# Row-wise dot products of two 64 MB tensors and a softmax: the last step's loads cut into eleven staggered pieces, three loads merged or re-cut, one SyncE drain added

## The chip, the cores and the metric

The kernel runs on one core of one Trainium2 chip. The metric is the device time of one execution in microseconds (us); several runs are taken and the median is given. The engines that matter are VectorE (DVE), ScalarE (ACT), SyncE (SP, which issues nearly all transfers) and the core's 16 DMA engines, which carry data from device memory into on-chip memory. A tile is a block of on-chip memory with 128 partitions.

## The reference

```
B, N, D = 8, 4096, 512
gram = np.matmul(x, y.transpose(0, 2, 1))
diag = np.diagonal(gram, axis1=1, axis2=2)
diag = diag - diag.max(axis=-1, keepdims=True)
exp = np.exp(diag)
return (exp / exp.sum(axis=-1, keepdims=True)).astype(np.float32)
```

Only the diagonal of the product is used, so for each of 8 x 4096 rows one dot product of 512 float32 elements of x and of y is needed, and then a softmax over the 4096 values of each of the 8 batches. All of x and y (2 x 67.1 MB) must be read once; the output is 0.13 MB.

## The kernel before

**Layout.** Four batches make one half (Q = 4). Each batch of a half takes 32 partitions (G = 32), and each partition holds 128 consecutive rows of x or y (C = 128). So `diag[0]` and `diag[1]`, one for each half, are tiles of 128 partitions x 128 dot products. `diag[1]` has one column more for a partial maximum.

**Steps.** The work runs in S = 8 steps of R = 32 rows per partition (four steps to each half); a step's x or y is 128 x 32 x 512 floats, 8.39 MB. There are two buffers for x (`xs[0]`, `xs[1]`, in turn) and one for y (`ys`), which the next step's y overwrites. Everything is issued in the order of the program: the schedule is written out by hand, each engine takes its instructions in that order, and semaphores are put in where one instruction needs another's result. An instruction that needs two of them has a separate semaphore wait in front of it on its engine.

**Steps 0 to 5** (line 118 on). SP loads x (`load_x`, line 63) and then y (`load_y`, line 66); step 0's x comes as two transfers, of 2 and of 30 rows. ACT copies the last K = 6 rows of `ys` to the tile `side` (line 123), so that `ys` is free sooner. DVE multiplies x by y in place (`products`, line 70): 26 rows against `ys`, then 6 rows against `side`. DVE then sums the products along D for 30 rows (`sums`, line 73), and ACT does the last two rows (`sums_act`, line 78, an activation with an accumulator for each row). The loads are held by the buffers: the next step's y waits until the products have read `ys`, the x of the step after next waits until the sums have read its buffer. After step 3 the first half's exponentials are made (`exps`, line 99); `normalize` (line 107) stands in step 4.

**Step 6** (lines 133 to 139). x in one transfer, y in two halves of 16 rows, with `products` for each half; DVE sums the last 8 rows and ACT the first 24.

**Step 7**, the last (lines 141 to 150). x and y come in pieces of 16, 8, 4, 2, 1 and 1 rows, in turn x and y; x's last piece has the last two rows, so that there are eleven transfers. `dots` (line 83) makes one row's dot product in one DVE instruction with an accumulator, for each row as its pieces land. Ahead of the dots of row 30, `largest` (line 97) takes the maximum of the 126 columns that are done into the extra column of `diag[1]`.

**The end** (lines 152 to 158). SP stores the first half's result `res[0]` in four transfers of 32 partitions. `exps` takes the maximum of the last three columns (the two last dots and the partial maximum), exchanges it over each group of 32 partitions (`over_quadrant`, line 91), ACT makes the exponentials and their sum, `normalize` sums over the groups, inverts and multiplies, and ACT issues the last store.

**Semaphores of the transfers.** All transfers share eight completion semaphores in turn, so the n-th waits until the (n - 8)-th has landed. SP waits for that in its own queue, with everything behind it.

**Ahead of step 0** (lines 115 and 116) `addr_align` fills DVE's and ACT's programs with no-operations up to an aligned address (61 each in the trace).

Of the kernel before, what the change touches and what calls it, by code (L numbers as in the profile page):

```python
# [1 line left out]

# [5 lines left out]


@with_exitstack
def kernel(
    ctx: ExitStack,
    tc: tile.TileContext,
    x: bass.AP,
    y: bass.AP,
    out: bass.AP,
):
    nc = tc.nc
    ctx.enter_context(tc.manual_schedule())  # L20
    f32 = mybir.dt.float32
    Alu = mybir.AluOpType
    Act = mybir.ActivationFunctionType
    X = mybir.AxisListType.X
    B, N, D = x.shape
    P = nc.NUM_PARTITIONS
    G = 32
    Q = P // G
    C = N // G
    R = 32  # L30
    H = R // 2
    K = 6
    W = 2
    S = B // Q * (C // R)


    xv = x.rearrange("(s b) (j c) d -> s (b j) c d", b=Q, j=G)
    yv = y.rearrange("(s b) (j c) d -> s (b j) c d", b=Q, j=G)
    ov = out.rearrange("(s b) (j c) -> s (b j) c", b=Q, j=G)

    big = ctx.enter_context(tc.tile_pool(name="big", bufs=1))
    small = ctx.enter_context(tc.tile_pool(name="small", bufs=1))


    xs = [big.tile([P, R, D], f32, name=f"xs{i}") for i in range(2)]
    ys = big.tile([P, R, D], f32, name="ys")
    side = big.tile([P, K, D], f32, name="side")

    diag = [small.tile([P, C + i], f32, name=f"diag{i}") for i in range(B // Q)]
    res = [small.tile([P, C], f32, name=f"res{i}") for i in range(B // Q)]  # L50

    def columns(t, r0, n):
        c0 = t % (C // R) * R + r0
        return slice(c0, c0 + n)

    def rows(t, r0, n):
        return xs[t % 2][:, r0 : r0 + n, :]

    def dots_of(t, r0, n):
        return diag[t * R // C][:, columns(t, r0, n)]  # L60

    def load_x(t, r0, n):
        nc.sync.dma_start(out=rows(t, r0, n), in_=xv[t * R // C, :, columns(t, r0, n), :])  # L63

    def load_y(t, r0, n):
        nc.sync.dma_start(out=ys[:, r0 : r0 + n, :], in_=yv[t * R // C, :, columns(t, r0, n), :])  # L66

    def products(t, r0, n, yt):
        xt = rows(t, r0, n)
        nc.vector.tensor_tensor(out=xt, in0=xt, in1=yt, op=Alu.mult)  # L70

    def sums(t, r0, n):
        nc.vector.tensor_reduce(out=dots_of(t, r0, n), in_=rows(t, r0, n), axis=X, op=Alu.add)  # L73

    def sums_act(t, r0, n):
        for r in range(r0, r0 + n):
            row = xs[t % 2][:, r, :]
            nc.scalar.activation(out=row, in_=row, func=Act.Copy, accum_out=dots_of(t, r, 1))  # L78

    def dots(t, r0, n):  # L80
        for r in range(r0, r0 + n):
            xt = xs[t % 2][:, r, :]
            nc.vector.scalar_tensor_tensor(  # L83
                out=xt, in0=xt, scalar=1.0, in1=ys[:, r, :], op0=Alu.mult, op1=Alu.mult,
                accum_out=dots_of(t, r, 1),
            )

    def over_quadrant(name, column, op, negate=False):

        got = small.tile([P, 1], f32, name=name)  # L90
        nc.vector.tensor_reduce(  # L91
            out=got, in_=column.to_broadcast([P, G]), axis=X, op=op, negate=negate, apply_transpose=True
        )
        return got

    def largest(out, d):
        nc.vector.tensor_reduce(out=out, in_=d, axis=X, op=Alu.max)  # L97

    def exps(i, d):
        mxp = small.tile([P, 1], f32, name=f"mxp{i}")  # L100
        largest(mxp, d)
        nmx = over_quadrant(f"nmx{i}", mxp, Alu.max, negate=True)
        sump = small.tile([P, 1], f32, name=f"sump{i}")
        nc.scalar.activation(out=res[i], in_=diag[i][:, :C], func=Act.Exp, bias=nmx, scale=1.0, accum_out=sump)  # L104
        return sump

    def normalize(i, sump):
        total = over_quadrant(f"sum{i}", sump, Alu.add)
        rc = small.tile([P, 1], f32, name=f"rc{i}")
        nc.vector.reciprocal(out=rc, in_=total)  # L110
        nc.vector.tensor_single_scalar(out=res[i], in_=res[i], scalar=rc, op=Alu.mult)  # L111

    nc.vector.addr_align(128, offset=0, max_nops=255)
    nc.scalar.addr_align(128, offset=0, max_nops=255)

    for t in range(S - 2):
        if t == 0:
            load_x(t, 0, 2)  # L120
        load_x(t, 2 if t == 0 else 0, R - 2 if t == 0 else R)
        load_y(t, 0, R)
        nc.scalar.activation(out=side, in_=ys[:, R - K :, :], func=Act.Copy)  # L123
        if t == C // R:
            normalize(0, sump)
        products(t, 0, R - K, ys[:, : R - K, :])
        products(t, R - K, K, side)
        sums(t, 0, R - W)
        sums_act(t, R - W, W)
        if t == C // R - 1:  # L130
            sump = exps(0, diag[0])

    t = S - 2
    load_x(t, 0, R)
    for r0 in (0, H):
        load_y(t, r0, H)
        products(t, r0, H, ys[:, r0 : r0 + H, :])
    sums(t, R - H // 2, H // 2)
    sums_act(t, 0, R - H // 2)

    t += 1
    r0 = 0
    for n in (16, 8, 4, 2, 1, 1):
        if r0 < R - 1:
            load_x(t, r0, max(n, 2))
        load_y(t, r0, n)
        if r0 == R - 2:
            largest(diag[1][:, C:], diag[1][:, : C - 2])
        dots(t, r0, n)
        r0 += n  # L150

    met = small.tile([P, C - R], f32, name="met")
    nc.scalar.activation(out=met, in_=diag[1][:, : C - R], func=Act.Copy)  # L153

    for p, n in ((0, G), (G, G), (2 * G, G), (3 * G, G)):
        nc.sync.dma_start(out=ov[0, p : p + n, :], in_=res[0][p : p + n, :])
    normalize(1, exps(1, diag[1][:, C - 2 :]))
    nc.scalar.dma_start(out=ov[1], in_=res[1])


# [1 line left out]
_INS = ['x', 'y']  # L162
_OUTS = [((8, 4096), 'float32')]


# [23 lines left out]
```

## Time and profile before

| what | value |
|---|---|
| time, median of 3 runs | 320.78 us (320.74 to 320.86) |
| profiled execution: span from first to last instruction | 318.9 us |
| time outside the span (median less span) | 1.9 us |
| bytes read from device memory | 134.22 MB, 421 GB/s over the span |
| DVE busy | 244.7 us (77%), 96 instructions |
| ACT busy | 42.0 us (13%), 84 instructions |
| longest idle of DVE for one cause | 66.5 us in 6 waits, for y |

The span is that of one execution, taken by the hardware profiler; time within it is counted from its first instruction. A line such as `L83 DVE SCALAR_TENSOR_TENSOR xs<-xs,ys 128x512` gives the code line, the engine, the operation, the tiles written and read and their shape. "SPq" is SP's queue: the time there is that of issuing a transfer, not of the transfer.

### The profile page before, as it was taken

The page shows a single profiled execution, that of the slowest core. Times are in us where ns is not written, and L with a number is a line of the kernel's source. Part 1 is how long each engine was busy: PE and PEld are TensorE (multiplying, and loading weights), DVE is VectorE, ACT ScalarE, POOL GpSimd, SP SyncE. Part 2 cuts the span into 40 slices and gives each one's busy share as a digit, 9 for nine tenths or more (in the row PEclk, how much of TensorE's full clock was granted, in tenths as well). Part 3 has the DMA queues.
Part 4 walks back from the last instruction along what each step waited for, and adds up shares of the span by engine and source line. Part 5 has one row for each costly group of instructions (what it writes and reads, how often), then busy time and mean ns, then how long its engine had stood idle before and what let it go on. Part 6 is the DMA issues. An engine that isn't in the chain of part 4 may idle for free.

```text
span 318.9 us, 424 instructions
## 1 busy us (share of the span) xinstructions
DVE 244.7 (77%) x96; ACT 42.0 (13%) x84; POOL 0.2 (0%) x4
## 2 busy tenths in 40 slices
DVE  0000069995899939999399994999949999996995
ACT  1000030100301003010120103000030100197000
POOL 0000000000000000000000000000000000000000
DMA  8999999999999999999999999999999899999993
GB/s 344 463 395 493 411 395 493 427 395 427 477 411 395 460 460 395 395 518 403 395 501 419 395 444 477 395 395 518 403 395 493 362 452 419 444 427 415 419 413 117
DMA packets 4226, 134.37 MB, mean 421 GB/s; under 512 B 512, under 2 KB 768, under 8 KB 1536
## 3 DMA queue, kind: packets, MB, share of 16 engines
q1 hardware_dynamic: 4080, 134.29, 97.9%
q10 hardware_dynamic: 144, 0.07, 0.1%
q14 instruction: 2, 0.02, 0.0%
HBM read 134.22 MB, written 0.13 MB: 421 GB/s over the span
## 4 chain that ended last, share of the span: by engine, by line
DMA 62%; DVE 35%; issue 2%; SPq 0%; ACT 0%; DVEq 0%
DMA ys<-in_y_dram 62%; DVE xs L70 30%; DVE diag L73 4%; DVE xs L83 0%; SPq L63 0%; DVE res L111 0%; DVE nmx L91 0%; DVE sum L91 0%; ACT res L104 0%; DVE rc L110 0%; DVE mxp L97 0%; DVEq L70 0%; SPq L66 0%; DVEq L83 0%
## 5 line engine op out<-in xcount | busy, mean ns | idle before, releaser
L70 DVE TENSOR_TENSOR xs<-xs,ys 128x13312 f32<-128x13312 f32 (+1 forms) x8 | 101.4, 12690 | 66.5 <-DMA ys<-in_y_dram 66.5
L73 DVE TENSOR_REDUCE diag<-xs 128x30 f32<-128x15360 f32 (+1 forms) x7 | 101.3, 14476 | 0.2
L78 ACT ACTIVATE xs<-xs 128x512 f32<-128x512 f32 x36 | 22.2, 617 | 111.0 <-DVE xs L70 111.0
L123 ACT ACTIVATE side<-ys 128x3072 f32<-128x3072 f32 x6 | 16.6, 2763 | 121.7 <-DMA ys<-in_y_dram 121.7
L83 DVE SCALAR_TENSOR_TENSOR xs<-xs,ys 128x512 f32<-128x512 f32 x32 | 19.9, 685 | 3.4 <-DMA ys<-in_y_dram 3.3
L70 DVE TENSOR_TENSOR xs<-xs,side 128x3072 f32<-128x3072 f32 x6 | 20.1, 3351 | 0.0
L78 ACT ACTIVATION_READ_ACCUMULATOR xs<-xs 128x1 f32 x36 | 6.7, 187 | 0.0
L104 ACT ACTIVATE res<-diag,nmx 128x128 f32<-128x128 f32 x2 | 0.8, 402 | 37.6 <-DVE nmx L91 37.6
L83 DVE DVE_READ_ACCUMULATOR xs<-xs,ys 128x1 f32 x32 | 2.6, 80 | 0.0
L123 ACT ACT_TABLE_LOAD x1 | 1.3, 1283 | 3.4 <-issue 3.4
L91 DVE TRANSPOSE_TENSOR_REDUCE sum<-sump 128x1 f32<-128x32 f32 x2 | 0.4, 211 | 1.2 <-ACT res L104 1.2
L111 DVE TENSOR_SCALAR res<-res,rc 128x128 f32<-128x128 f32 x2 | 0.6, 288 | 0.1
L97 DVE TENSOR_REDUCE mxp<-diag 128x1 f32<-128x128 f32 (+1 forms) x2 | 0.4, 222 | 0.1
L91 DVE TRANSPOSE_TENSOR_REDUCE nmx<-mxp 128x1 f32<-128x32 f32 x2 | 0.4, 212 | 0.1
L110 DVE RECIPROCAL rc<-sum 128x1 f32<-128x1 f32 x2 | 0.3, 163 | 0.1
L104 ACT ACTIVATION_READ_ACCUMULATOR res<-diag,nmx 128x1 f32 x2 | 0.4, 188 | 0.0
L97 DVE TENSOR_REDUCE diag<-diag 128x1 f32<-128x126 f32 x1 | 0.3, 284 | 0.1
L153 ACT ACTIVATE met<-diag 128x96 f32<-128x96 f32 x1 | 0.3, 283 | 0.0
L173 POOL MEMSET const-bfloat16-1.0<- 128x1 bf16 x1 | 0.1, 102 | 0.0
L173 POOL MEMSET const-uint8-127<- 128x1 uint8 x1 | 0.1, 102 | 0.0
L173 POOL MEMSET const-float32-0.0<- 128x1 f32 x1 | 0.1, 99 | 0.2 <-issue 0.2
L173 POOL MEMSET const-float32-1.0<- 128x1 f32 x1 | 0.1, 99 | 0.0
## 6 DMA issues: line engine op xcount, KB each, us to landing
ys<-in_y_dram SPq DMA_DIRECT2D x3, 4096.0 KB, 16.0
xs<-in_x_dram SPq DMA_DIRECT2D x1, 7680.0 KB, 21.8
xs<-in_x_dram SPq DMA_DIRECT2D x1, 4096.0 KB, 14.9
xs<-in_x_dram SPq DMA_DIRECT2D x1, 2048.0 KB, 20.5
ys<-in_y_dram SPq DMA_DIRECT2D x1, 2048.0 KB, 17.2
xs<-in_x_dram SPq DMA_DIRECT2D x3, 512.0 KB, 22.1
xs<-in_x_dram SPq DMA_DIRECT2D x1, 1024.0 KB, 19.3
ys<-in_y_dram SPq DMA_DIRECT2D x1, 1024.0 KB, 21.3
```

The costliest lines, as they stand in the source:

```text
L70: nc.vector.tensor_tensor(out=xt, in0=xt, in1=yt, op=Alu.mult)
L73: nc.vector.tensor_reduce(out=dots_of(t, r0, n), in_=rows(t, r0, n), axis=X, op=Alu.add)
L78: nc.scalar.activation(out=row, in_=row, func=Act.Copy, accum_out=dots_of(t, r, 1))
L83: nc.vector.scalar_tensor_tensor(out=xt, in0=xt, scalar=1.0, in1=ys[:, r, :], op0=Alu.mult, op1=Alu.mult, accum_out=dots_of(t, r, 1),)
L91: nc.vector.tensor_reduce(out=got, in_=column.to_broadcast([P, G]), axis=X, op=op, negate=negate, apply_transpose=True)
L97: nc.vector.tensor_reduce(out=out, in_=d, axis=X, op=Alu.max)
L104: nc.scalar.activation(out=res[i], in_=diag[i][:, :C], func=Act.Exp, bias=nmx, scale=1.0, accum_out=sump)
L110: nc.vector.reciprocal(out=rc, in_=total)
L111: nc.vector.tensor_single_scalar(out=res[i], in_=res[i], scalar=rc, op=Alu.mult)
L123: nc.scalar.activation(out=side, in_=ys[:, R - K :, :], func=Act.Copy)
L153: nc.scalar.activation(out=met, in_=diag[1][:, : C - R], func=Act.Copy)
L173: nc = _bacc.Bacc("TRN2", target_bir_lowering=False, num_devices=1)
```

## The change

It does the following.

- A `drain` on SP stands ahead of step 0's loads.
- Step 0's x is loaded in one transfer.
- Step 6's y is loaded in one transfer. `side` now takes step 6's first six rows of y; the products are made of rows 6 to 16, then of rows 17 to 31, then of rows 0 to 5 with `side`. DVE sums three rows (0 to 2), ACT the other 29.
- Step 7's eleven transfers are, in order: x 15 rows, y 17, x 8, y 8, x 5, y 4, x 2, y 2, x one and a half rows, y one row, and x's last 256 columns of row 31. Rows 0 to 30 are one dot each, as soon as x and y are there. Row 31 is two instructions of 256 columns: the first puts its sum into one more column of `xs[1]`, behind row 31; the second covers the last 256 columns and that column, which is multiplied by a 1.0 that a `memset` has put behind row 31 in `ys`. So the first half's sum is added by the second's accumulator.
- The partial maximum of 127 columns stands behind row 30's dot and ahead of row 31's two halves.
- `res[0]` is stored in six transfers (32, 32, 16, 16, 16 and 16 partitions).
- The tiles are flat; `xs[1]` and `ys` have one more float in each partition.

```diff
     K = 6
     W = 2
+    F = 17
+    V = 3
...
-    xs = [big.tile([P, R, D], f32, name=f"xs{i}") for i in range(2)]
-    ys = big.tile([P, R, D], f32, name="ys")
-    side = big.tile([P, K, D], f32, name="side")
+    xs = [big.tile([P, R * D + i], f32, name=f"xs{i}") for i in range(2)]
+    ys = big.tile([P, R * D + 1], f32, name="ys")
+    side = big.tile([P, K * D], f32, name="side")
...
-    def rows(t, r0, n):
-        return xs[t % 2][:, r0 : r0 + n, :]
+    def rows(tile_, r0, n):
+        return tile_[:, r0 * D : (r0 + n) * D].rearrange("p (r d) -> p r d", d=D)
...
+    def load(tile_, view, t, r0, n):
+        nc.sync.dma_start(out=rows(tile_, r0, n), in_=view[t * R // C, :, columns(t, r0, n), :])
...
-    def dots(t, r0, n):
-        for r in range(r0, r0 + n):
-            xt = xs[t % 2][:, r, :]
-            nc.vector.scalar_tensor_tensor(
-                out=xt, in0=xt, scalar=1.0, in1=ys[:, r, :], op0=Alu.mult, op1=Alu.mult,
-                accum_out=dots_of(t, r, 1),
-            )
+    def dot(t, e0, n, got):
+        xt = xs[t % 2][:, e0 : e0 + n]
+        nc.vector.scalar_tensor_tensor(
+            out=xt, in0=xt, scalar=1.0, in1=ys[:, e0 : e0 + n], op0=Alu.mult, op1=Alu.mult, accum_out=got
+        )
...
+    nc.sync.drain()
 
     for t in range(S - 2):
-        if t == 0:
-            load_x(t, 0, 2)
-        load_x(t, 2 if t == 0 else 0, R - 2 if t == 0 else R)
+        load_x(t, 0, R)
         load_y(t, 0, R)
...
     t = S - 2
     load_x(t, 0, R)
-    for r0 in (0, H):
-        load_y(t, r0, H)
-        products(t, r0, H, ys[:, r0 : r0 + H, :])
-    sums(t, R - H // 2, H // 2)
-    sums_act(t, 0, R - H // 2)
+    load_y(t, 0, R)
+    nc.scalar.activation(out=side, in_=ys[:, : K * D], func=Act.Copy)
+    products(t, K, F - K, rows(ys, K, F - K))
+    products(t, F, R - F, rows(ys, F, R - F))
+    products(t, 0, K, rows(side, 0, K))
+    sums(t, 0, V)
+    sums_act(t, K, R - K)
+    sums_act(t, V, K - V)
 
     t += 1
-    r0 = 0
-    for n in (16, 8, 4, 2, 1, 1):
-        if r0 < R - 1:
-            load_x(t, r0, max(n, 2))
-        load_y(t, r0, n)
-        if r0 == R - 2:
-            largest(diag[1][:, C:], diag[1][:, : C - 2])
-        dots(t, r0, n)
-        r0 += n
+    E = R * D
+    half = E - D // 2
+    nc.vector.memset(ys[:, E : E + 1], 1.0)
+    x1, y1, done = 0, 0, 0
+    for n, m in ((15, F), (8, 8), (5, 4), (2, 2)):
+        load_x(t, x1, n)
+        x1 += n
+        while done < min(x1, y1):
+            dot(t, done * D, D, dots_of(t, done, 1))
+            done += 1
+        load_y(t, y1, m)
+        y1 += m
+        while done < min(x1, y1):
+            dot(t, done * D, D, dots_of(t, done, 1))
+            done += 1
+    last = xv[t * R // C].rearrange("p c d -> p (c d)")
+    o = columns(t, 0, R).start * D
+    nc.sync.dma_start(out=xs[t % 2][:, x1 * D : half], in_=last[:, o + x1 * D : o + half])
+    load_y(t, y1, R - y1)
+    nc.sync.dma_start(out=xs[t % 2][:, half:E], in_=last[:, o + half : o + E])
+    while done < R - 1:
+        dot(t, done * D, D, dots_of(t, done, 1))
+        done += 1
+    largest(diag[1][:, C:], diag[1][:, : C - 1])
+    dot(t, (R - 1) * D, D // 2, xs[t % 2][:, E:])
+    dot(t, half, D // 2 + 1, dots_of(t, R - 1, 1))
...
-    for p, n in ((0, G), (G, G), (2 * G, G), (3 * G, G)):
+    for p, n in ((0, G), (G, G), (2 * G, 16), (2 * G + 16, 16), (3 * G, 16), (3 * G + 16, 16)):
         nc.sync.dma_start(out=ov[0, p : p + n, :], in_=res[0][p : p + n, :])
-    normalize(1, exps(1, diag[1][:, C - 2 :]))
+    normalize(1, exps(1, diag[1][:, C - 1 :]))
```

## The prediction, made before the changed kernel ran

> **What bounds the kernel now.** First the page's slices, then busy time by stretch.
>
> ```profile
> DVE  0000069995899939999399994999949999996995
> DMA  8999999999999999999999999999999899999993
> ```
> ```profile
> 42.00:81.00 39.00, 33.45 (x3) 4.10 (x5) 0.00 (x0) 1.00 1.00 430
> ...
> 265.00:294.00 29.00, 26.03 (x4) 15.10 (x49) 0.00 (x0) 1.00 1.00 428
> 294.00:313.30 19.30, 18.88 (x61) 0.00 (x0) 0.00 (x0) 1.00 1.00 412
> 313.00:319.00 6.00, 2.50 (x10) 0.50 (x2) 0.00 (x0) 1.00 0.08 24
> ```
>
> The columns of the second fence are length, busy time of DVE, ACT and POOL, clock, DMA share, GB/s. DMA is at 0.97 to 1.00 of its time from start to 313 us, while DVE has some 5 us to spare in each step. So the kernel is one stream of 134 MB, then a tail. In the last stretch ahead of the tail DVE is full too (18.88 of 19.30 us): there both run side by side.
>
> Next the chain of waits at the end, and the timeline over the same time.
>
> ```profile
> 278.04 16.00 DMA ys<-in_y_dram
> 294.04 0.02 issue
> 294.06 19.27 DMA ys<-in_y_dram
> 313.33 0.03 issue
> ...
> 313.42 1.32 DVE xs L83 x4
> 314.74 0.02 issue
> 314.77 0.17 DVE mxp L97
> ```
> ```profile
> 312.87 0.28 DVE L97 TENSOR_REDUCE diag<-diag 128x1 f32<-128x126 f32 x1
> 313.42 0.69 DVE L83 SCALAR_TENSOR_TENSOR xs<-xs,ys 128x512 f32<-128x512 f32 x1 [0.26 <-DMA ys<-in_y_dram]
> 314.04 0.08 DVE L83 DVE_READ_ACCUMULATOR xs<-xs,ys 128x1 f32 x1
> 314.04 0.69 DVE L83 SCALAR_TENSOR_TENSOR xs<-xs,ys 128x512 f32<-128x512 f32 x1
> 314.65 0.08 DVE L83 DVE_READ_ACCUMULATOR xs<-xs,ys 128x1 f32 x1
> 314.77 0.16 DVE L97 TENSOR_REDUCE mxp<-diag 128x1 f32<-128x3 f32 x1
> ```
>
> Row 30's y lands at 313.33 and releases two dots; row 31's y lands at 313.93 by its semaphore, while row 30's dot still runs, so it holds up nothing. From the maximum (`mxp`) at 314.77 to the end, 4.13 us, is one chain that the change leaves alone; so are the 1.9 us outside the span.
>
> **The stream, part by part.** The transfers' semaphores, read from the trace, give landings 19.35 us apart for a whole 32 rows (235.84 to 255.19), 9.72 and 9.70 for step 6's two halves of y, 1.28 or 1.29 for two rows, and 0.67 and 0.60 for the last two single rows; 0.605 us a row, and 0.03 to 0.08 for each cut.
>
> - Step 6's y in one: 19.42 becomes 19.35, **-0.06**.
> - Step 0's x in one. In the records of the DMA packets the first starts at 1.75; 4096-byte packets take 0.159 each, a 65,536-byte one 2.418, so eight small ones cost 0.06 more than their share of large ones. But the first small ones took up to 0.54, and the engines turned to the second transfer only after some 1.5 us, where eight take 1.24. How much of that start a large packet hides no row shows: between -0.04 and -0.4; I take **-0.15**, nearer the packets' own rate.
> - The drain. SP's drains at the program's end take 7 ns and stand 0.06 ahead of the next instruction. Nothing is on its way yet, and the first load is behind it: **+0.06**, 0 to 0.2.
> - Step 7: eleven transfers before and after, cut elsewhere: **0**, within 0.1. The flat tiles and the two extra floats move `ys` in memory. Packets that start 4096 bytes into a tile move as many bytes per ns as those from its start (61,440 in 2.267, 65,536 in 2.418): 0; if y's packets lost 0.2% of their 155 us, +0.3.
>
> The sum is -0.15: the stream ends at 313.78 instead of 313.93. Counted back by 0.33 for half a row and 0.64 for a row, x's one and a half rows land at **312.81**, y's last row at 313.45.
>
> **DVE before the tail.** A product takes 14.03 us for 13,312 columns and 3.35 for 3072, so 1.042 ns each and 0.15, starts 0.09 ahead of its forerunner's end. Step 6's y lands at 274.5; DVE, idle since 269.4, is busy with 11, 15 and 6 rows (5.94, 8.08, 3.38) and three rows of sums (1.75) until 293.75, and with the memset (0.1, as POOL's) until 293.85. Step 7's first 17 rows of y are due at 293.9: nothing lost, with no room either. From there dots go at 0.613 each (294.14, 294.76, 295.37 in the trace). Rows 15, 17, 23, 25 and 28 find their pieces landed; row 29 waits for y until 311.85, ends at 312.5, and DVE is idle until 312.81. So 0.3 us late at the start would still be made up there. The side copy (2.76) is over at 277.4, and its product comes 11 us later; ACT's 29 rows at 0.613 end by 299.8, while DVE's partial maximum needs them at 313.6. Of the six stores the last is issued when the one-and-a-half-row transfer has landed; it takes some 2 us beside a last store that starts at 316.5. None of this is on the path.
>
> **The tail.** Behind 312.81 on DVE: a wait of 0.05; row 30's dot 0.61 and its accumulator 0.08; a gap of 0.10 and the maximum, 0.28, as at 312.77 to 313.15; the first half dot (256 x 1.042 + 0.08 by the dots' spacing) 0.35 and its accumulator 0.08; the second half, which needs that accumulator, 0.04 to 0.10 later, 0.35 and 0.08; and 0.04 to `mxp`. That is 2.02, or 1.87 to 2.15 with the small gaps all short or all long: `mxp` at **314.83** against 314.77. From the last landing (313.78) alone it would be 314.3: the last 256 columns are not what the end waits for. What lands last is made smaller, but the partial maximum, hidden in a wait before (0.28), comes onto the path, and one dot becomes two that hang together.
>
> No row has two dots of which the second reads the first's accumulator; the nearest is `mxp` behind the last dot (0.04) and the partial maximum behind row 29's (0.10). The Trainium skill's page "VectorE: DVE Perf Modes", in "The DRAIN you can't avoid", has it that a semaphore between VectorE instructions costs nothing extra; its "Rules for kernel authors" advise to save instructions, not semaphores. By it the second half would follow 0.35 us after the first, the tail would be 1.85, and the time 0.17 less. In this trace independent dots start before their forerunner has ended, dependent instructions after its accumulator: I go by the rows.
>
> **Sum.** 318.9 - 0.15 for the stream + 0.21 for the longer tail behind it = 318.96; with 1.9 outside, against the median of 320.78, **320.84**, in its own right 320.3 to 321.3. Less than 0.2% (0.64 us) is about what a measurement of this kernel can't tell from no change.
>
> **Rivals.**
>
> 1. **A gap in the stream ahead of step 7's y (slower).** Its first 17 rows overwrite rows 6 to 16, which the first product of step 6 reads until 280.66; SP can issue it at 280.73, and all of SP's later loads stand behind it. Step 7's x ends at 283.6, so the lead is 2.9 us, where the trace has 6.3 (issue at 278.04, x's landing 284.32) and 5.1 in the steps before. The packets of x end some 0.45 ahead of its landing, at 283.2. The first transfer of all has its packets 1.02 to 1.70 after its issue: then no gap, with 0.8 us to spare on the slowest DMA engine. From 2.5 us on, the stream stops. At 3.2 it would lose 0.7, all of it carried to the end: **321.55**. For it speaks that no transfer in the full stream was issued so late; against it, the one start seen. Chance 0.17.
> 2. **DVE late in step 7 (slower).** If step 6's three products or the waits between the groups of dots cost 1.1 us more than summed (or y's packets are slower), DVE doesn't meet row 30's x, 0.3 is made up and 0.8 stays: **321.65**. For it: DVE has a margin of 0.1 at 293.85. Against it: all durations are rows of this trace, within 0.05. Chance 0.08.
> 3. **The start was worth more (faster).** The instruction queue's two packets of 8 KB at 8 us and the slow first packets put two of the 16 DMA engines 0.46 behind the third-last at the end of step 0's x (22.41 and 22.51 against 22.05), and 0.23 are left at 254.7. If one large transfer takes away 0.4 and the packets fall where they delay nobody (0.25), and the tail's gaps are all short (0.15), it is **320.05**. Chance 0.15.
> 4. **The end follows the last 256 columns,** as the last piece's size suggests: `mxp` at 314.3, 320.3. It would need row 30's x half a microsecond earlier than what lies ahead of it allows; it is within the forecast's range.
>
> **How the numbers follow.** The forecast (with 4) has 0.60, all within 0.2% (320.14 to 321.42). Rivals 1 and 2 are slower, 0.25. Rival 3 gives 0.13 faster and 0.02 within. Faster 0.13, same 0.62, slower 0.25. The range runs from 320.1, just short of rival 3, to 321.7, over rivals 1 and 2.
>
> **What would show it.** Right: step 0's x lands ahead of 22.96, by 0.1 to 0.2; step 6's y 19.35 after its x; SP issues step 7's first y near 280.7 and it lands 10.3 after x's 15 rows; DVE waits for row 30's x and for nothing after it; `mxp` 2.0 after that landing. Wrong: DMA slices below 9 near 283 and landings that all shift from there (rival 1); DVE without a wait ahead of row 30 (2); step 0's x 0.4 earlier (3); a wait of the second half dot for the last piece (4).

## The result, and the profile after

| | before | changed |
|---|---|---|
| time, median | 320.78 us (320.74 to 320.97, 6 runs) | 322.77 us (321.44 to 323.20, 6 runs) |
| span of the profiled execution | 318.9 us | 321.4 us |

The ratio is 1.0055, with a 95% interval of 1.0041 to 1.007: the change makes the kernel 0.4 to 0.7% slower. It also makes it uneven: the runs before lie within 0.2 us, those after within 1.8. The profiled execution, from which this section's lines are, is the slowest of the six (323.20). The forecast of 320.84 is wrong, and so is its range.

The slices of the changed kernel first, in the same form as before:

```profile
DVE  0000079994899939999399995999769995896995
DMA  9999999999999999999999999999999999999991
GB/s 393 393 424 481 400 416 473 416 391 489 424 391 489 424 391 473 440 391 473 440 391 473 440 391 473 440 391 465 440 400 440 465 400 407 436 359 407 428 409 50
```

The DMA line looks perfect: busy all the way. The loss shows only in the line below it: the 36th slice, 281 to 289 us, moved 359 GB/s. A DMA engine counts as busy while a packet is under way, however slowly it comes. One low slice proves little, though. The same line of the kernel before has a 362 (the 32nd):

```profile
GB/s 344 463 395 493 411 395 493 427 395 427 477 411 395 460 460 395 395 518 403 395 501 419 395 444 477 395 395 518 403 395 493 362 452 419 444 427 415 419 413 117
```

There 493 and 452 stand on either side and make it up, 436 on the mean of the three; the changed kernel's 359 has 436 and 407 beside it, a mean of 401. So the stretch around it, for the kernel before and for the changed one (length, busy time of DVE, ACT and POOL, clock, DMA share, GB/s):

```profile
282.00:292.00 10.00, 9.03 (x2) 10.00 (x33) 0.00 (x0) 1.00 1.04 446
```
```profile
42.00:274.00 232.00, 201.84 (x23) 25.13 (x32) 0.00 (x0) 1.00 1.00 432
...
282.00:292.00 10.00, 10.00 (x2) 8.79 (x31) 0.00 (x0) 1.00 0.96 369
```

Up to 274 us the changed kernel streams at 432 GB/s, as before. Then 369 GB/s for ten microseconds, where the kernel before has 446 (a packet is put down where it starts, which makes short stretches uneven). Which transfer that was, the issues on SP and the table of issues with their time to landing tell:

```profile
269.58 0.33 SPq L64 DMA_DIRECT2D xs<-in_x_dram  x1
280.87 0.33 SPq L64 DMA_DIRECT2D ys<-in_y_dram  x1
281.24 0.43 SPq L64 DMA_DIRECT2D xs<-in_x_dram  x1
```
```profile
ys<-in_y_dram SPq DMA_DIRECT2D x1, 4352.0 KB, 15.7
xs<-in_x_dram SPq DMA_DIRECT2D x1, 3840.0 KB, 14.2
```

Step 7's x of 15 rows lands at 269.58 + 14.2 = 283.8. Its first y, 17 rows, is issued at 280.87, so 2.9 us ahead of that, and lands at 280.87 + 15.7 = 296.5: by the semaphores 12.74 us after x, where 17 rows take 10.3 at the full rate. These **2.4 us** are the loss in this execution. All later landings follow at the full rate (4.85 and 4.90 for the two transfers of 8 rows, 3.08 for 5, 2.52 for 4), so nothing is lost elsewhere in the stream.

The chain of waits at the end (start, length, what) doesn't name that transfer:

```profile
291.20 0.04 issue
291.25 24.10 DMA xs<-in_x_dram
315.35 0.02 issue
315.37 0.71 DVE xs L86 x2
```

It goes from row 30's dot to the transfer that released it (x's one and a half rows) and back to its issue at 291.25. All that this transfer stood behind in the queue, the slow y first of all, is in those 24.10 us; a chain through a queue has to be read together with the landings ahead. The end itself, by the timeline:

```profile
315.07 0.08 DVE L86 DVE_READ_ACCUMULATOR xs<-xs,ys 128x1 f32 x1
315.37 0.69 DVE L86 SCALAR_TENSOR_TENSOR xs<-xs,ys 128x512 f32<-128x512 f32 x1 [0.22 <-DMA xs<-in_x_dram]
315.99 0.08 DVE L86 DVE_READ_ACCUMULATOR xs<-xs,ys 128x1 f32 x1
316.18 0.28 DVE L99 TENSOR_REDUCE diag<-diag 128x1 f32<-128x127 f32 x1
316.38 0.42 DVE L86 SCALAR_TENSOR_TENSOR xs<-xs,ys 128x256 f32<-128x256 f32 x1
316.72 0.08 DVE L86 DVE_READ_ACCUMULATOR xs<-xs,ys 128x1 f32 x1
316.84 0.43 DVE L86 SCALAR_TENSOR_TENSOR xs<-xs,ys 128x257 f32<-128x257 f32 x1
317.19 0.08 DVE L86 DVE_READ_ACCUMULATOR xs<-xs,ys 128x1 f32 x1
317.31 0.15 DVE L99 TENSOR_REDUCE mxp<-diag 128x1 f32<-128x2 f32 x1
```

DVE waits for row 30's x (landing 315.35) and for no transfer after it, and the last maximum comes 1.96 later. The last 256 columns land at 316.37, well ahead of the instruction that needs them (316.84).

### The profile page after: what moved, and what is told of

The parts are those of the page before. It is cut to its first block, busy times and chain, and to the rows that moved or that the text cites. A ratio compares the mean times of both kernels' runs of the same rounds, so it can differ in the third digit from the quotient of the medians.

```text
span 321.4 us, 435 instructions
## 1 busy us (share of the span) xinstructions
DVE 242.3 (75%) x100; ACT 48.0 (15%) x95; POOL 0.2 (0%) x4
## 4 chain that ended last, share of the span: by engine, by line
DMA 66%; DVE 31%; SPq 1%; issue 1%; ACT 0%; DVEq 0%
DMA ys<-in_y_dram 59%; DVE xs L74 31%; DMA xs<-in_x_dram 7%; SPq L64 1%; DVE xs L86 0%; DVE res L113 0%; DVE diag L99 0%; DVE nmx L93 0%; DVE sum L93 0%; ACT res L106 0%; DVE rc L112 0%; DVE mxp L99 0%; DVEq L74 0%; DVEq L99 0%; SPq L119 0%
## 5 line engine op out<-in xcount | busy, mean ns | idle before, releaser
L74 DVE TENSOR_TENSOR xs<-xs,ys 128x13312 f32<-128x13312 f32 (+2 forms) x8 | 98.2, 12291 | 71.9 <-DMA ys<-in_y_dram 71.9
L77 DVE TENSOR_REDUCE diag<-xs 128x30 f32<-128x15360 f32 (+1 forms) x7 | 98.7, 14096 | 0.2
L82 ACT ACTIVATE xs<-xs 128x512 f32<-128x512 f32 x41 | 25.3, 618 | 92.1 <-DVE xs L74 92.1
L124 ACT ACTIVATE side<-ys 128x3072 f32<-128x3072 f32 x6 | 16.6, 2767 | 121.8 <-DMA ys<-in_y_dram 121.8
L74 DVE TENSOR_TENSOR xs<-xs,side 128x3072 f32<-128x3072 f32 x7 | 23.5, 3351 | 0.0
L86 DVE SCALAR_TENSOR_TENSOR xs<-xs,ys 128x512 f32<-128x512 f32 (+2 forms) x33 | 20.0, 669 | 3.0 <-DMA ys<-in_y_dram 2.7
L82 ACT ACTIVATION_READ_ACCUMULATOR xs<-xs 128x1 f32 x41 | 7.7, 188 | 0.0
L137 ACT ACTIVATE side<-ys 128x3072 f32<-128x3072 f32 x1 | 2.8, 2766 | 20.0 <-DMA ys<-in_y_dram 20.0
## 6 DMA issues: line engine op xcount, KB each, us to landing
ys<-in_y_dram SPq DMA_DIRECT2D x1, 4352.0 KB, 15.7
xs<-in_x_dram SPq DMA_DIRECT2D x1, 3840.0 KB, 14.2
```

What stands on the lines that cost most here:

```text
L77: nc.vector.tensor_reduce(out=dots_of(t, r0, n), in_=rows(xs[t % 2], r0, n), axis=X, op=Alu.add)
L86: nc.vector.scalar_tensor_tensor(out=xt, in0=xt, scalar=1.0, in1=ys[:, e0 : e0 + n], op0=Alu.mult, op1=Alu.mult, accum_out=got)
L124: nc.scalar.activation(out=side, in_=ys[:, (R - K) * D : R * D], func=Act.Copy)
L137: nc.scalar.activation(out=side, in_=ys[:, : K * D], func=Act.Copy)
```

## The experiments

The theory after the result: **late issue**. Step 7's first y may be issued only when the product of step 6 that reads its rows is done; with 2.9 us of transfer left ahead of it the DMA engines run out of work and come back slowly. Rivals: the transfers of 15 and 17 rows are slow in themselves (**cut**), or the altered work of step 6 on DVE and ACT slows the loads (**company**). "Loss" below is y's landing less that of the x before it, less what its rows take at the full rate (10.3 for 17 rows, 9.71 for 16). Each time stands beside runs of the kernel before on the same chip.

### 1. Step 6's y in two transfers again (the single load undone)

```diff
-    load_y(t, 0, R)
-    nc.scalar.activation(out=side, in_=ys[:, : K * D], func=Act.Copy)
-    products(t, K, F - K, rows(ys, K, F - K))
-    products(t, F, R - F, rows(ys, F, R - F))
-    products(t, 0, K, rows(side, 0, K))
-    sums(t, 0, V)
-    sums_act(t, K, R - K)
-    sums_act(t, V, K - V)
+    load_y(t, 0, F)
+    products(t, 0, F, rows(ys, 0, F))
+    load_y(t, F, R - F)
+    products(t, F, R - F, rows(ys, F, R - F))
+    sums(t, R - 8, 8)
+    sums_act(t, 0, R - 8)
```

> Three theories of the 2.4 us that step 7's first y (17 rows) lost after step 7's first x (15 rows): LATE: it was issued with only 2.9 us of transfer ahead of it. CUT: transfers of 15 and 17 rows are slow in themselves. COMPANY: what DVE and ACT do in the changed step 6 slows the loads. Here step 6's y is again two transfers (17 and 15 rows) with a product for each, DVE sums 8 rows and ACT 24; step 7 is as changed. So the first y of step 7 is issued near 278.7, 5.1 us ahead of the landing of the x before it. LATE and COMPANY: it lands 10.3 us after that x, and the time is 320.7 to 321.1. CUT: it lands 11 to 13 after, and the time is 321.5 to 323.2.

Measured: 321.11 beside 321.07, ratio 1.0004 (0.9995 to 1.0013); 321.11 is 0.01 over the range given for late issue and company, where **cut** has at least 321.5. The issues on SP and the stretch:

```profile
270.04 0.33 SPq L64 DMA_DIRECT2D xs<-in_x_dram  x1
279.17 0.33 SPq L64 DMA_DIRECT2D ys<-in_y_dram  x1
```
```profile
282.00:292.00 10.00, 9.63 (x3) 10.00 (x34) 0.00 (x0) 1.00 1.02 441
```

x lands at 284.32, so y is issued 5.2 us ahead, and the same 17 rows behind the same 15 land 10.32 later: no loss, 441 GB/s. That takes away **cut** as a cause by itself. Late issue and company are both left, since step 6's work went back too.

### 2. The kernel before, made late

```diff
-    for r0 in (0, H):
-        load_y(t, r0, H)
-        products(t, r0, H, ys[:, r0 : r0 + H, :])
+    load_y(t, 0, H)
+    load_y(t, H, H)
+    for r0, n in ((0, 10), (H, 6), (10, 6), (H + 6, 10)):
+        products(t, r0, n, ys[:, r0 : r0 + n, :])
```

> The kernel before with the order of step 6's products alone changed (rows 0 to 9, 16 to 21, 10 to 15, 22 to 31), so that step 7's first y (16 rows, after an x of 16 rows) is issued near 281.4 instead of 278.0, with 2.9 us of transfer ahead of it instead of 6.3. LATE: it lands 10.7 to 12.2 us after that x instead of 9.7, and the time is 321.7 to 323.3. CUT and COMPANY: it lands 9.7 after, and the time is 320.7 to 321.0.

Measured: 321.66 beside 321.07, ratio 1.0018 (1.0008 to 1.0027); the profiled execution took 322.08.

```profile
281.88 0.33 SPq L66 DMA_DIRECT2D ys<-in_y_dram  x1
```
```profile
282.00:292.00 10.00, 9.67 (x2) 8.78 (x29) 0.00 (x0) 1.00 0.98 406
```

x lands at 284.83 and y is issued 2.96 us ahead. It lands 10.62 after x, so the loss is 0.9. Landing and time lie just under what late issue expected (10.7 and 321.7); the other two expected no loss. The later issue alone makes the kernel before slower, with its own sizes and nearly its own work.

### 3. The changed kernel's first y in 6 and 11 rows

```diff
-        load_y(t, y1, m)
+        if y1 == 0:
+            load_y(t, 0, K)
+            load_y(t, K, m - K)
+        else:
+            load_y(t, y1, m)
         y1 += m
```

> The changed kernel with step 7's first y in two transfers: rows 0 to 5, which need ACT's copy alone and are issued near 277.6, 6.2 us ahead of the landing of the x before, and rows 6 to 16, issued near 280.9 with 6.5 us of transfer ahead. LATE: both land within 10.5 us of that x, time 320.7 to 321.2. CUT: the same, since no transfer of 17 rows is left. COMPANY: the loss of 0.7 to 2.5 us stays, time 321.5 to 323.2.

Measured: 321.12 beside 321.07, ratio 1.0002 (0.9992 to 1.0011).

```profile
ys<-in_y_dram SPq DMA_DIRECT2D x1, 2816.0 KB, 13.4
...
ys<-in_y_dram SPq DMA_DIRECT2D x1, 1536.0 KB, 9.9
```
```profile
282.00:292.00 10.00, 10.00 (x2) 8.78 (x30) 0.00 (x0) 1.00 1.00 426
```

The six rows that ACT's copy frees go out at 277.63, 6.2 us ahead of x's landing; they keep the engines fed while DVE frees the other eleven (issue 280.90). Both land within 10.40 us of x. Step 6 is that of the changed kernel, so **company** falls as the cause. With one more transfer the whole loss is gone.

### 4. Sixteen and sixteen rows: a lead between the two

```diff
-    F = 17
+    F = 16
-    for n, m in ((15, F), (8, 8), (5, 4), (2, 2)):
+    for n, m in ((16, F), (7, 9), (5, 4), (2, 2)):
```

> The changed kernel with step 7 begun by 16 rows of x and 16 of y (then 7, 9, 5, 4 and so on), and step 6's first product of rows 6 to 15. The first y is issued near 280.3, with 4.0 us of transfer ahead of it instead of 2.9. LATE: a smaller loss than 2.4 or none, y lands 9.7 to 10.7 after that x, time 320.8 to 321.8. CUT: none, 320.8 to 321.1. COMPANY: the loss stays, 321.5 to 323.2.

Measured: 321.14 beside 321.07, ratio 1.0003 (0.9993 to 1.0012). The lead was 4.06, y landed 10.08 after x: a loss of 0.4, as late issue has it. In the time it can't be told from none.

### 5. The changed kernel again

> The changed kernel unaltered, beside the others on one chip. LATE (step 7's first y is issued with 2.9 us of transfer ahead of it; the DMA engines run dry and come back slowly): the loss is there again, another size in each execution as in its first six runs, 0.7 to 2.5 us; time 321.5 to 323.2. A rival, CHIP: the loss belonged to the chip or the day of the first runs; then 321.0 to 321.3, as the two variants whose first y was issued earlier.

Measured: 322.37 (322.02 to 323.07) beside 320.76, ratio 1.0051 (1.0037 to 1.0064); in the profiled execution y landed 12.60 after x. The loss belongs to the kernel, not to the chip of the first runs.

### 6 and 7. The tail and the start, with the loss taken away

Both start from the variant with 6 and 11 rows. The first:

```diff
+    largest(diag[1][:, C:], diag[1][:, : C - 2])
     while done < R - 1:
         dot(t, done * D, D, dots_of(t, done, 1))
         done += 1
-    largest(diag[1][:, C:], diag[1][:, : C - 1])
...
-    normalize(1, exps(1, diag[1][:, C - 1 :]))
+    normalize(1, exps(1, diag[1][:, C - 2 :]))
```

> The changed kernel with step 7's first y in two transfers (6 and 11 rows, as in the run of that name) and the partial maximum moved ahead of row 30's dot, over 126 columns; the last maximum takes three columns again. TAIL (in the change the partial maximum stands on the path, 0.28 and a gap of 0.10): the maximum is hidden in DVE's wait for row 30's x, the last maximum comes 1.6 us after that x's landing instead of 2.0, and the time is 0.2 to 0.4 below the 321.12 of the variant without it (on that chip). RIVAL: the end then waits for x's last 256 columns (landing, 0.05, 0.43, 0.04: 1.5 us after row 30's x), which leaves 0.3 to 0.4 too, or DVE has no wait of 0.3 there and nothing is won.

Measured: 320.69 beside 320.76, ratio 0.9995 (0.9987 to 1.0004). Its timeline:

```profile
313.14 0.28 DVE L99 TENSOR_REDUCE diag<-diag 128x1 f32<-128x126 f32 x1
313.34 0.68 DVE L86 SCALAR_TENSOR_TENSOR xs<-xs,ys 128x512 f32<-128x512 f32 x1
...
314.88 0.15 DVE L99 TENSOR_REDUCE mxp<-diag 128x1 f32<-128x3 f32 x1
```

Row 30's x lands at 313.29, so the last maximum comes 1.59 after it instead of 1.96: the partial maximum is under DVE's wait again. The trace shows the 0.37; against the kernel before, on two chips, the ratio went from 1.0002 to 0.9995, which the intervals don't separate. The second restores the start:

```diff
-    nc.sync.drain()
...
-        load_x(t, 0, R)
+        if t == 0:
+            load_x(t, 0, 2)
+        load_x(t, 2 if t == 0 else 0, R - 2 if t == 0 else R)
         load_y(t, 0, R)
```

> The variant before, with the start as before the change: no drain, step 0's x as 2 and 30 rows. As predicted for the change: the start by one transfer is worth 0.15 and the drain costs 0.06, so this is 0.1 slower than the variant with the drain and one transfer. As its trace has it (first x landed 0.16 later with one transfer, and in the first microseconds fewer GB/s were moved): 0.1 to 0.2 faster.

Measured: 320.70 beside 320.76, ratio 0.9999 (0.999 to 1.0008): no difference from 320.69, so neither reading is confirmed by the time. The first x landed at 23.13 (two transfers) and 23.29 (one).

### 8. The kernel before, made later still

As in 2, with 9 rows in the place of 6: products of rows 0 to 9, 16 to 24, 10 to 15, 25 to 31.

> The kernel before with step 6's products in the order rows 0 to 9, 16 to 24, 10 to 15, 25 to 31, so that step 7's first y (16 rows) is issued near 283.1, with 1.3 to 1.5 us of transfer ahead of it (2.96 in the run with 6 rows in the place of 9, which lost 0.9). LATE: a larger loss, y lands 11 to 13 us after the x before instead of 9.7, time 322 to 324. RIVAL, ORDER (the altered order of the products slows the loads, not the late issue): the loss is as in that run, 0.5 to 1.2, time 321.5 to 322.2.

Measured: 321.82 beside 320.76, ratio 1.0032 (1.0019 to 1.0044).

```profile
283.04 0.33 SPq L66 DMA_DIRECT2D ys<-in_y_dram  x1
```
```profile
282.00:288.00 6.00, 5.97 (x3) 4.95 (x17) 0.00 (x0) 1.00 0.72 279
```

With a lead of 1.34 the engines are visibly empty (DMA share 0.72), and y lands 10.69 after x: a loss of 1.0, hardly more than the 0.9 at 2.96. So the expectation of late issue, "the later, the more", is missed, and by its numbers the run meets the rival, order. But order would have the loads slowed, and the packets show a gap: the sixteen engines end x between 282.87 and 283.91 and begin y between 284.00 and 285.06, and stand idle for 1.2 us on the mean in between. That gap is the late issue's. That the order costs nothing besides, no run shows.

### 9, 10 and 12. What sets the size

Experiment 9 begins the changed kernel with 14 and 16 rows (F = 16, then 9 and 9, 5 and 4), 10 begins the kernel before with 15 and 17 (products of rows 0 to 9, 16 to 20, 10 to 15, 21 to 31; then 9 and 7, 4 and 4, 2 and 2), and 12 is 4 with a product of rows 16 and 17 ahead of that of rows 6 to 15. All have a lead of 2.9.

> What is open: the changed kernel (17 rows of y after 15 of x, 2.9 us ahead) loses 2.3 to 2.5 in its profiled executions, the kernel before with 16 rows, as late, 0.9. Theories: SIZE (a first y of more than 32,768 bytes in a partition comes back slower once the engines have run dry), FRAME (what else runs in the changed step 6 makes it worse). Here the changed kernel begins step 7 with 14 rows of x and 16 of y (then 9, 9, 5, 4), step 6's first product is of rows 6 to 15, the lead is 2.9 us. SIZE: a loss of 0.5 to 1.2, y 10.2 to 10.9 us after x, time 321.0 to 321.9. FRAME: 1.7 to 2.5, y 11.4 to 12.2 after x, time 322 to 323.

> The kernel before with step 6's products in the order rows 0 to 9, 16 to 20, 10 to 15, 21 to 31 and step 7 in pieces of 15, 9, 4, 2, 2 rows of x and 17, 7, 4, 2, 1, 1 of y, so that its first y has 17 rows with 2.9 us ahead of it. SIZE: y lands 12 to 13 us after x instead of 10.3, time 322 to 323. FRAME: 10.9 to 11.5 after, time 321.2 to 322.0.

> Still open is what sets the size of the loss at one and the same lead. This is the variant with 16 rows of x and 16 of y (lead 4.06, which lost 0.4) with a product of rows 16 and 17 ahead of that of rows 6 to 15, so that the first y is issued 2.9 us ahead of the landing of the x before: as late as in the run with 14 and 16 rows (y landed 1.2 later than at full rate, median time 1.6 over the kernel before) and as in the kernel before with 16 and 16 (0.9 and 0.6). FRAME (the changed step 6): as the former, y 10.7 to 11.4 us after x, time 322.0 to 322.7 where the kernel before takes 320.8. CUT (the sizes of the two transfers): as the latter, y 10.1 to 10.7 after x, time 321.3 to 321.8. Under either, more than the 0.4 of the lead of 4.06.

| rows of x, y | frame | loss in the profiled execution | median, and beside it the kernel before |
|---|---|---|---|
| 16, 16 (2) | before | 0.9 | 321.66, 321.07 |
| 15, 17 (10) | before | 2.0 | 322.61, 320.83 |
| 14, 16 (9) | changed | 1.2 | 322.44, 320.83 |
| 16, 16 (12) | changed | 1.5 | 322.44, 320.79 |
| 15, 17 (5) | changed | 2.3 | 322.37, 320.76 |

10 met the expectation of size by its landing and time; 9's landing (10.91) lies just above that of size, below that of frame, and its time is that of frame; 12 met frame. Neither explains the five alone. That a lead of 2.9 us loses in all five is shown; what decides between 0.9 and 2.4 stays **open**. Each loss in the table is that of one execution, and the runs of one kernel differ by 0.7 to 1.8 us, as much as the rows do. By the medians, 10, 9, 12 and 5 lose alike, 1.6 to 1.8 us over the kernel before, and only 2 loses less, 0.6.

### 11. The changed kernel, made later still

```diff
+    products(t, F, 3, rows(ys, F, 3))
     products(t, K, F - K, rows(ys, K, F - K))
-    products(t, F, R - F, rows(ys, F, R - F))
+    products(t, F + 3, R - F - 3, rows(ys, F + 3, R - F - 3))
```

> The changed kernel with a product of rows 17 to 19 ahead of that of rows 6 to 16, so that the first y of step 7 (17 rows) is issued near 282.5, 1.3 us ahead of the landing of the x before, instead of 2.9. LATE as first stated (the later, the more): a loss over 2.5, time over 323. EMPTY (all engines run dry for a microsecond and start together, as in the kernel before with the lead of 1.34, which lost 1.0; worse is a start in which some engines come back while others still run): a loss of 1.0 to 1.8, so no larger than the changed kernel's, and the landings of the engines lie closer together afterwards (spread near 0.5 us instead of 2.7).

Measured: 322.25 (322.08 to 322.28) beside 320.83, ratio 1.0046 (1.0028 to 1.0064).

```profile
ys<-in_y_dram SPq DMA_DIRECT2D x1, 4352.0 KB, 12.9
xs<-in_x_dram SPq DMA_DIRECT2D x1, 3840.0 KB, 14.2
```

Issued at 282.50, 1.25 us ahead, y lands at 295.4, 11.6 after x: a loss of 1.3, less than the 2.4 and 2.3 of the changed kernel's profiled executions, which issue 1.6 us **earlier**. In the time the two can't be told apart (322.25 here, 322.37 in 5). Counting the packets under way in the trace's records, by microseconds:

```
                         282   283   284   285   286   287   288
changed, engines busy   14.9  12.8  14.6  16.0  15.9  15.9  16.0   (of 16)
changed, GB/s            374   303   356   328   309   381   415
later (11), busy         9.3   5.6  15.3  16.0  16.1  16.0  16.1
later (11), GB/s         247   106   288   363   435   432   433
```

In the changed kernel few engines are ever idle, together 5.7 us or 0.4 for each of the sixteen; what costs more is that for some three microseconds, 285 to 288, all sixteen work slowly (packets of 34,816 bytes take up to 2.44 us instead of 1.29). In experiment 11 nearly all fall idle, 1.1 us on the mean, then start together, and are at the full rate two microseconds later. Afterwards the engines' landings of one transfer lie 0.69 us apart, in the changed kernel 2.75, and a transfer has landed only when its slowest engine has. So "empty" met its expectation.

The mean of the sixteen engines' landings tells the other half: by it y is late by 1.6 us in 11 and 1.3 in the changed kernel, by 1.5 in 8 and 0.5 in 2. The later issue does cost the mean engine more; the slowest engine, by which the kernel goes on, it costs no more, since the engines end closer together. Why a half-empty stream scatters its engines and an empty one doesn't, no run shows.

## Why the prediction was wrong

- **The step that failed** is the first rival's bound, which gave the late first y a price of 0: "The first transfer of all has its packets 1.02 to 1.70 after its issue: then no gap, with 0.8 us to spare on the slowest DMA engine. From 2.5 us on, the stream stops." The issue time (280.87 against 280.73) was right, and so was the first packet of y: it runs at 282.14, 1.27 after the issue. But the bound comes from the start of the program, where nothing runs, and doesn't hold behind a running transfer. In the records of the packets, ten of the sixteen engines go on from x to y within 0.01 us. The six others end x between 282.36 and 282.96 and get their first packet of y between 282.68 and 284.9, from 1.8 to some 4 us after the issue; in 5 it is six again, 2.4 to 3.4 us after. (In experiment 1, with a lead of 5.2, all sixteen go on within 0.01 us.) Then the rate stays low for microseconds after all are back, which the bound had no term for. The 0.8 us were also those of the wrong engine: the engines end x between 282.14 and 283.31, and 1.70 after the issue, 282.57, is later than the first to end.
- **The price.** The place, the mechanism (a gap ahead of that y) and its direction stood in that rival, with a chance of 0.17 and a time of 321.55; the loss measured is 2.4 in the profiled execution, not the 0.7 it was given. The shallower lead was known (2.9 against 5.1 and 6.3 in the trace); no row showed such a lead, and the bound should have run from 0 up to the loss of a restart.
- **The sum of the rest** is not contradicted. With the late issue mended (3), the change is worth nothing that can be measured: ratio 1.0002 (0.9992 to 1.0011), where 320.84 against 320.78 was forecast. The interval is some 0.3 us to either side, and each term is smaller than that, so the agreement doesn't confirm them one by one; they are read from the traces below.
- **Step 6's y in one transfer**: 19.36 from x's landing to y's instead of 19.42, as predicted (19.35).
- **Step 0's x in one transfer**: -0.15 forecast; not found. One transfer landed between 23.08 and 23.33 in nine executions, two transfers between 22.96 and 23.47 in five, and the times of 6 and 7 are equal. The rate over the microseconds from 2 to 6 was 313, 353, 361, 421 GB/s in the changed kernel, with one transfer of large packets, and 292, 406, 433, 434 in the kernel before, with two small rows ahead. From 4 to 5 it is 343 to 374 in all nine executions with one transfer and 414 to 434 in all five with two. So what was taken for a delay that a large packet hides is a slow start, and with large packets it lasts longer. It looks like the slow rate behind the late y; that both have one cause is not shown.
- **The drain**: 0.05 to 0.06, as predicted (the first load at 0.78 instead of 0.73).
- **DVE**: step 6's sums ended 19.24 after y's landing against 19.25, the memset took 0.06 instead of 0.1, and the wait ahead of row 30 was 0.22 (0.28 in 3) against 0.3. So no term of this part failed.
- **The tail**: 1.96 against 2.02, and "the last 256 columns are not what the end waits for" holds. That it comes so close is partly luck: the terms listed add up to 2.06 to 2.12, since the sum leaves out the gap ahead of the second half dot (0.04 to 0.10, measured 0.04); and the first half dot starts 0.08 before the maximum has ended, which no term had. The second half dot starts 0.46 after the first, where 0.35 was the estimate for two that don't depend on each other: it waits for the first one's accumulator, which is read from 0.34 on for 0.08, and starts 0.04 later. The Trainium skill's page "VectorE: DVE Perf Modes", in "The DRAIN you can't avoid", would have it, from a run of copies, that a semaphore costs nothing extra; here the dependence costs 0.11, and the measurement decides.
- **Rivals 2, 3 and 4** did not occur: DVE has its wait ahead of row 30, step 0's x is not earlier, and the second half dot waits for no transfer.

## What to carry to other kernels

In a kernel that is one stream of loads, look at how far ahead of the running transfer's landing the next one is issued. Here 5 us lost nothing, 4 lost 0.4, 2.9 between 0.9 and 2.4, and 1.3 between 1.0 and 1.3, each in one profiled execution. A time from issue to first packet that was read where nothing ran is no bound for a transfer behind a running one. Where a buffer comes free late, split the load so that a part which is free early goes out first; and read GB/s over some ten microseconds, or the landings, not the busy share, to see whether a stream is full.

## What the runs showed of the hardware that was not expected

- A lead that is longer than the time from issue to first packet at the program's start (1.0 to 1.7 us) isn't enough to keep the rate of 432 GB/s: behind a running transfer, six of the changed kernel's sixteen engines got their first packet from 1.8 to some 4 us after the issue. The Trainium skill's page "DMA: Bandwidth & Descriptors", in "Anatomy of one DMA", gives a fixed cost of about 2.0 us per transfer, measured on the GpSimd path; by it, as an estimate, 2.9 us would have been ample. The runs on SP's queue show a loss at 2.9 in five kernels and at 4.06 in one, so here the measurement goes further than the page.
- The loss of the landing doesn't grow with the delay: 2.4 and 2.3 at a lead of 2.9, 1.3 at 1.25; in the kernel before 0.9 at 2.96, 1.0 at 1.34. The mean over the engines does: 1.3 and 1.6, 0.5 and 1.5.
- All sixteen DMA engines can be busy for microseconds while they move 309 to 381 GB/s (285 to 288 us in the changed kernel), where 432 is the full rate.
